# Feed-forward tiles moved to byte 288 of 512, and two weight halves exchanged between the ring of halves and the ends of the form tiles

## The chip, the cores and the metric

The kernel runs on one core of one Trainium2 chip. The metric is device time in microseconds; the kernel before takes 1804.18 us (median of 3 runs, 1803.63 to 1804.41).

## The reference

One encoder block over 256 tokens of width 2048. Two gated branches (a chunked linear attention and a Hyena convolution) are merged, projected and normalized; then comes the part that the change touches, a feed-forward layer with hidden width 8192:

```python
h  = _layernorm(ALPHA * h + mix, ln1_g, ln1_b)
ff = jnp.square(jax.nn.relu(h @ w_ff1)) @ w_ff2      # 2048 -> 8192 -> 2048
h  = _layernorm(ALPHA * h + ff, ln2_g, ln2_b)
```

All is float32 outside. Inside, each operand is split into a high part (rounded to the matmul format, made by ScalarE) and a low part (the rest, made by VectorE), and a product is taken as high x high + high x low + low x high.

## The kernel before

**Stages.** Input projections, the two branches, merging and output projection fill the first 1100 us. The feed-forward layer is cut into four quarters of 2048 hidden channels (16 blocks of 128 each).

- `ff1_first` makes the first quarter: 16 channel blocks `f0_*`. Each is one `[128 weights x 128]` load after the other, with the activations `hT` streamed past them (`channel_products`, lines 139 to 152): 8 products of 512 columns with the high half `h=0` (line 147), 16 of 256 columns with the low parts (line 151), and 8 of 512 with the high half `h=1`.
- `ff_pairs` is a loop of 48 iterations `s`. In each, TensorE forms the second layer's products of a finished pair of blocks (`form_products`, lines 1243 to 1245) and one channel block `f` of the next quarter. The second layer is taken by a seven-product scheme (quarters of the weight block are added up in pairs, and so are the activations). One iteration on TensorE, in order, is 9 products of the plain units (`w0` to `w2`), 6 of the pair (`w3`, `w4`), the channel block (8 + 16 + 8 products), then 6 of the last units (`w5`, `w6`) of the iteration before.
- Behind the loop, the last quarter's second layer is taken plainly (`token_products`, lines 199 to 201), with the activations as stationary operand, while `ff_close` finishes the seven-product sums.

**Operands of the products.** In a channel block the stationary operand is a weight half and the moving one is `hT`. In `form_products` the stationary operand is a slot of `fa[0]` or `fa[1]` (activation forms; four slots of 1792 floats each, slots 0 to 3 in `fa[0]`, 4 to 7 in `fa[1]`), and the moving one is a weight unit of 512 floats:

```python
for k, (wh, wl) in zip(ks, pieces_of.pop((p, which))):
    ps, f = pss[k], FORM[k]
    sh, sl = slot[:, 0, f], slot[:, 1, f]
    pin(MM(ps, sh, wh, start=(i == 0), stop=False))     # L1243
    MM(ps, sh, wl, start=False, stop=False)             # L1244
    pin(MM(ps, sl, wh, start=False, stop=(i == 7)))     # L1245
```

**Where the weights lie.** `weight_half(n, h)` takes a pair of tiles (`whi`, `wlo`, 1024 floats each) from a ring of three. In `ff_pairs` each iteration uses the ring three times: `half_split(s+1, 0)`, `pair_split(s+1)`, `half_split(s+1, 1)`. `plain_split` writes its units to `b_h` (tile `xh`) and `b_l` (tile `wx`). `last_split(s)` writes units 1 and 2, which POOL's accumulating DMAs have made into sums in the raw tile `ring`, to the ends `[:, 7168:8192]` of `fa[0]` (high) and `fa[1]` (low). VectorE's and ScalarE's order in the loop is written out by hand (`pin`). After the loop `fetch` puts blocks of the last quarter through the same ring; there the order is left to a planner.

The loop's body, in the order that is written out (lines 1286 to 1310):

```python
form_products(pss, s, 0, (0, 1, 2)); form_products(pss, s, 1, (3, 4))
ps = channel_psum(...)
for h in range(2): channel_products(ps, hT, half_parts.pop((s, h)), ...)
if s: form_products(pss, s - 1, 2, (5, 6))
if s + 2 < SLOTS: ring_load(s + 2)
if more: plain_split(s + 1); half_split(s + 1, 0); pair_split(s + 1)
...                                  # take_sums, squares, forms
quad_sum(n, c, ps, ...)              # low <- f on ScalarE, then fr <- f, f_l on VectorE
if more: half_split(s + 1, 1)
last_split(s)
```

**Addresses.** The pool `ep` lays its tiles one behind the other in the order in which their tags first appear: `bst` (384 bytes), `wx` (4096), `xh` and `xl` (8192 each), `f` (32768), `hT` (32768), then twelve buffers of 32 bytes for the norms' small columns (`mv`, `rs_y`, `rs_t`, `rs_v`, `lrs`, `lnb`, two each), then `fr3`, `fr4`, `ft`, `fraw`. The start of each large operand within a partition, modulo 512 bytes, follows:

| tile | start modulo 512 |
|---|---|
| `xT`, later `mT`, later `fa[0]`; `yT`, later `yg`, `yh` | 288 |
| `whi`, `wlo` (ring of halves), `raw`, `ring`, `dfth`, `eoh`, `Yh` | 32 |
| `hx` (Hyena filters) | 64 |
| `wx` (`b_l`), `xh` (`b_h`), `xl`, `f` (later `fa[1]`), `hT` | 416 |
| `fraw` | 288 |

All slots, units and weight columns used as operands lie at whole multiples of 512 bytes from these starts.

Of the kernel before, what the change touches and what calls it, by code (L numbers as in the profile page):

```python
# [9 lines left out]
F32 = mybir.dt.float32  # L10
# [6 lines left out]
P = 128  # L17
# [13 lines left out]
FF_PAIRS = W_OUT_END + 16  # L31
# [12 lines left out]
def block_kernel(  # L44
# [63 lines left out]
    def weight_half(n, h):  # L108
        return (wp.tile([P, D // 2], F32R, tag="whi", bufs=3, name=f"whi{n}_{h}"),
                wp.tile([P, D // 2], F32R, tag="wlo", bufs=3, name=f"wlo{n}_{h}"))  # L110
# [138 lines left out]
    with tc.tile_pool(name="xp", bufs=1) as xp, tc.tile_pool(name="xq", bufs=1) as xq:  # L249
# [25 lines left out]
        for i in range(3):  # L275
            t = weight_half(-1, i)
# [17 lines left out]
        for k0, n in PIECES:  # L294
# [13 lines left out]
            if k0 == 0:  # L308
                hi, lo = places[0]
# [165 lines left out]
    for i in range(2 * NCH):  # L475
        c, o = divmod(i, 2)
        n = 4 + (i * 21) // 15
# [421 lines left out]
    ep = ctx.enter_context(tc.tile_pool(name="ep", bufs=1))  # L899
# [4 lines left out]
    def load_rows(i0):  # L904
        rows = zr[:, 2:4]
        for i in range(2):
            nc.scalar.dma_start(rows[:, i, :], ln_rows[i0 + i:i0 + i + 1, :].broadcast_to([P, D]))
        return rows
# [54 lines left out]
                            MM(ps, sl, hi[:, cs], start=False, stop=(kt == KT - 1))  # L963

    st1 = ep.tile([P, NT, 8, 6], F32, tag="bst", name="bst1")
    rows1 = load_rows(0)
    turn_b, turn_i = dfth, dftl
    for i, t in ((0, turn_b), (1, turn_i)):
# [104 lines left out]
    fa = [base.tile([P, 8192], F32R, tag="xT", name="fa0"), None]  # L1073

    def fa_slot(i):
        if fa[1] is None:
            fa[1] = ep.tile([P, 8192], F32R, tag="f", name="fa1")
        t = fa[i // 4][:, i % 4 * 1792:(i % 4 + 1) * 1792]
        return t.rearrange("p (h k j) -> p h k j", h=2, j=P)
# [24 lines left out]
    def cast(hi, src):  # L1104
        return pin(nc.scalar.copy(hi, src))  # L1105

    def rest(lo, src, hi):
        return VT(lo, src, hi.bitcast(F32), ALU.subtract)
# [64 lines left out]
    def split_units(p, kind, hi, lo, raw):  # L1173
        by_unit = [t.rearrange("p (u c) -> p u c", c=512) for t in (hi, lo)]
        cast(by_unit[0], raw)
        rest(by_unit[1], raw, by_unit[0])
        pieces_of[p, kind] = list(zip(units(hi), units(lo)))

    def raw_units(p):
        return ring_tile(p).rearrange("p (u c) -> p u c", c=512)  # L1180
# [3 lines left out]
        split_units(p, 1, hi, lo, raw_units(p)[:, 0:4:3])  # L1184

    def last_split(p):
        fa_slot(4)
        hi, lo = (t[:, 7168:8192] for t in fa)
        split_units(p, 2, hi, lo, raw_units(p)[:, 1:3])

    block_raw = [None, None]
# [1 line left out]
    def block_load(p):  # L1193
        if block_raw[p % 2] is None:
            block_raw[p % 2] = ep.tile([P, D], F32, tag=("xl", "fraw")[p % 2], name=f"fraw{p}")
        nc.sync.dma_start(block_raw[p % 2], wblk[FF_PAIRS + 1 + 2 * p])
# [1 line left out]
    half_parts = {}  # L1198

    def half_split(p, h):  # L1200
        hi, lo = weight_half(FF_PAIRS + 1 + 2 * p, h)
        src = block_raw[p % 2][:, h * 1024:(h + 1) * 1024]
        cast(hi, src)
        rest(lo, src, hi)
        half_parts[p, h] = (hi, lo)
        if h and p + 2 < SLOTS:
            block_load(p + 2)
# [71 lines left out]
    def ff_pairs():  # L1279
        pss = [psum_side(f"w{j}") if j not in (2, 3, 4) else psum_main(f"w{j}") for j in range(7)]  # L1280
        joins = []
        for s in range(SLOTS):
# [12 lines left out]
            if more:  # L1295
                plain_split(s + 1)
                half_split(s + 1, 0)
# [9 lines left out]
            if more:  # L1307
                half_split(s + 1, 1)
            last_split(s)
            take_sums(pss, s - 1, (5, 6))  # L1310
            if s == SLOTS - 7:
# [32 lines left out]
    for h in range(2):  # L1344
        half_split(0, h)
# [58 lines left out]
    with tc.high_priority(), tc.issue_after(done.ins):  # L1404
        add_ff(pss[1][:, 0:256], 1, 1792, 256, last=True)
        mv = ep.tile([P, 2], F32, tag="mv", bufs=2, name="mvl")
        nc.vector.bn_aggr(mv, st2[:, 1])
        y, t, v, rs = (ep.tile([P, 1], F32, tag=f"fin{i}", name=f"fin{i}") for i in range(4))
# [158 lines left out]
```

## Time and profile before

| | |
|---|---|
| median of 3 runs | 1804.18 us |
| the profiled execution | 1803.89 us |
| its span | 1802.1 us |
| granted TensorE clock | 0.999 |
| busy: TensorE / VectorE / ScalarE / POOL | 1793.6 / 1455.6 / 1039.2 / 164.6 us |

Times in the profile count from the start of the span. In the profile PE is the stream of matmuls and PEld that of weight loads; DVE is VectorE and ACT ScalarE. The mean of one matmul in a group counts from its start to its modelled end, and neighbours overlap in it. The chain of waits counts from one start to the next. A name like `w<-b_h,fa` is output, moving operand, stationary operand.

### The profile page before, as it was taken

What the parts mean: (1) busy time and instruction counts of PE and PEld (TensorE: products, weight loads), DVE (VectorE), ACT (ScalarE), POOL (GpSimd) and SP (SyncE); (2) the same over time, 40 slices, a digit from 0 to 9 for tenths busy, and PEclk for the clock granted to TensorE, in tenths of its full rate; (3) what the DMA queues carried; (4) which work ended last, traced back from release to release, by engine and by line L of the source; (5) the groups of instructions that cost most, each with busy time, mean ns of one, the idle gap of its engine ahead of it and who ended that gap; (6) DMA issues with size and microseconds to landing.
All of it is one profiled execution on the core that took longest, in us unless ns stands there. A gap on an engine that the chain in (4) does not pass through costs nothing.

```text
span 1802.1 us, 23458 instructions
## 1 busy us (share of the span) xinstructions
PE 1793.6 (100%) x8787; PEld 1506.8 (84%) x8787; DVE 1455.6 (81%) x1869; ACT 1039.2 (58%) x1399; POOL 164.6 (9%) x217
## 2 busy tenths in 40 slices
PE   9999999999999999999999999999999999999998
PEld 7888888888888888888888889888888888888887
DVE  6789887875679989998845568687899889999867
ACT  6678768875344444445544445666667666665632
POOL 1011110000111101010000000001111111111100
PEclk9999999999999999999999999999999999999999
DMA  8668775455797979798555764568888888888663
GB/s 325 231 248 293 253 234 196 149 179 197 224 311 247 276 261 285 232 309 257 202 187 187 283 236 155 203 192 258 243 252 255 249 243 261 247 240 276 212 222 119
DMA packets 79281, 424.76 MB, mean 236 GB/s; under 512 B 9816, under 2 KB 12392, under 8 KB 38464
## 3 DMA queue, kind: packets, MB, share of 16 engines
q1 hardware_dynamic: 47808, 336.61, 50.5%
q0 software_dynamic: 24304, 66.99, 18.1%
q10 hardware_dynamic: 7056, 19.67, 3.0%
q8 instruction: 69, 1.13, 0.3%
q14 instruction: 44, 0.36, 0.1%
HBM read 381.86 MB, written 16.25 MB: 221 GB/s over the span
## 4 chain that ended last, share of the span: by engine, by line
PE 97%; DVE 2%; issue 0%; ACT 0%; DVEq 0%; ACTq 0%
PE f L147 12%; PE f L151 6%; PE w L1244 4%; PE w L1243 4%; PE w L1245 4%; PE g L200 3%; PE g L199 3%; PE g L201 3%; PE ux L200 3%; PE ux L199 3%; PE ux L201 3%; PE r L199 2%; PE r L200 2%; PE r L201 2%; PE k L147 2%; PE v L200 2%
## 5 line engine op out<-in xcount | busy, mean ns | idle before, releaser
L86 ACT CAST whi<-raw 128x1024 fp32r<-128x1024 f32 x392 | 412.5, 1053 | 412.9 <-PE ux L201 85.1
L87 DVE TENSOR_TENSOR wlo<-raw,whi 128x1024 fp32r<-128x1024 f32 x392 | 478.4, 1223 | 206.9 <-ACT whi L86 204.6
L147 PE MATMUL f<-hT,whi 128*128 128x512 f32 x984 | 246.9, 395 | 0.4 <-DVE fr L1102 0.4
L147 PEld LDWEIGHTS f<-hT,whi 128*128 128x128 f32 x984 | 180.7, 188 | 38.8 <-DVE fr L1102 0.8
L151 PEld LDWEIGHTS f<-hT,wlo 128*128 128x128 f32 x984 | 125.4, 188 | 5.6
L1102 DVE TENSOR_TENSOR wlo<-fraw,whi 128x1024 fp32r<-128x1024 f32 x96 | 117.3, 1222 | 13.5 <-ACT whi L1105 11.2
L151 PE MATMUL f<-hT,wlo 128*128 128x256 f32 x984 | 127.0, 282 | 0.0
L1105 ACT CAST whi<-ring 128x1024 fp32r<-128x1024 f32 x48 | 50.6, 1054 | 101.0 <-DVE ring L1102 97.6
L1168 POOL DMA_DIRECT2D ring<-wblk x48 | 41.7, 868 | 706.9 <-DVE ring L1102 706.9
L1105 ACT CAST whi<-fraw 128x1024 fp32r<-128x1024 f32 x96 | 100.7, 1049 | 0.1
L200 PE MATMUL g<-wlo,xT 128*128 128x512 f32 x256 | 100.2, 391 | 0.0
L201 PE MATMUL ux<-whi,xT 128*128 128x512 f32 x256 | 99.9, 390 | 0.0
L201 PE MATMUL g<-whi,xT 128*128 128x512 f32 x256 | 99.9, 390 | 0.0
L200 PE MATMUL ux<-wlo,xT 128*128 128x512 f32 x256 | 99.7, 389 | 0.0
L199 PE MATMUL g<-whi,xT 128*128 128x512 f32 x256 | 93.8, 392 | 0.0
L1105 ACT CAST b_h<-ring 128x1024 fp32r<-128x1024 f32 x96 | 75.2, 832 | 25.9 <-PE w L1245 21.5
L199 PE MATMUL ux<-whi,xT 128*128 128x512 f32 x256 | 89.7, 389 | 0.0
L1102 DVE TENSOR_TENSOR b_l<-ring,b_h 128x1024 fp32r<-128x1024 f32 x48 | 58.7, 1223 | 16.0 <-ACT b_h L1105 15.9
L1102 DVE TENSOR_TENSOR ring<-ring 128x512 f32<-128x512 f32 x96 | 66.2, 689 | 1.5
L1102 DVE TENSOR_TENSOR wlo<-ring,whi 128x1024 fp32r<-128x1024 f32 x48 | 58.8, 1225 | 1.9 <-ACT whi L1105 0.3
L1102 DVE TENSOR_TENSOR fa<-ring,fa 128x1024 fp32r<-128x1024 f32 x48 | 58.5, 1220 | 0.0
L1169 POOL DMA_DIRECT2D ring<-ring x48 | 58.1, 1210 | 0.0
(537 smaller groups left out, 4305.9 us busy)
## 6 DMA issues: line engine op xcount, KB each, us to landing
raw<-wblk SPq DMA_DIRECT2D x204, 1024.0 KB, 5.0
fraw<-wblk SPq DMA_DIRECT2D x48, 1024.0 KB, 4.8
ring<-wblk SPq DMA_DIRECT2D x48, 1024.0 KB, 7.1
Td<-T POOLq DMA_DIRECT2D x32, 384.0 KB, 5.4
conv_sb<-conv_rows SPq DMA_DIRECT2D x12, 1024.0 KB, 11.5
Tl<-Td POOLq DMA_DIRECT2D x16, 768.0 KB, 9.5
ring<-wblk POOLq DMA_DIRECT2D x48, 256.0 KB, 4.4
ring<-ring POOLq DMA_DIRECT2D x48, 256.0 KB, 5.1
```

Source lines behind the costliest of these rows:

```text
L86: return (nc.scalar.copy(hi, src), nc.vector.tensor_tensor(lo, src, hi.bitcast(F32), op=ALU.subtract))
L87: nc.vector.tensor_tensor(lo, src, hi.bitcast(F32), op=ALU.subtract))
L147: MM(ps[:, :, ts], hi[:, js], act[:, kt, :, ts], start=(kt == 0 and opens), stop=(kt == KT - 1))
L151: MM(ps[:, 0, ts], lo[:, js], act[:, kt, 0, ts], start=False, stop=False)
L199: MM(pss[tb], sh, wh, start=(kt == 0), stop=False)
L200: MM(pss[tb], sh, wl, start=False, stop=False)
L201: MM(pss[tb], sl, wh, start=False, stop=(kt == KT - 1))
L1102: return pin(nc.vector.tensor_tensor(dst, a, b, op=op))
L1105: return pin(nc.scalar.copy(hi, src))
L1243: pin(MM(ps, sh, wh, start=(i == 0), stop=False))
L1244: MM(ps, sh, wl, start=False, stop=False)
L1245: pin(MM(ps, sl, wh, start=False, stop=(i == 7)))
```

## The change

Two edits. The first creates the twelve small buffers of the norms ahead of the large tiles of `ep` (behind `bst`), without any instruction: they take 12 x 32 = 384 bytes there, and everything from `wx` to `hT` starts 384 bytes later, at 288 modulo 512. The tiles behind them stay where they were. The second exchanges two places: `half_split(p, 1)`, the second half of a channel block's weights, goes to the ends of `fa[0]` and `fa[1]`, and `last_split(p)`, the DMA-made sums, goes to the ring of halves.

```diff
     st1 = ep.tile([P, NT, 8, 6], F32, tag="bst", name="bst1")
+    for tag, n in (("mv", 2), ("rs_y", 1), ("rs_t", 1), ("rs_v", 1), ("lrs", 1), ("lnb", 1)):
+        ep.tile([P, n], F32, tag=tag, bufs=2, name=f"first_{tag}")
     rows1 = load_rows(0)
...
     def last_split(p):
-        fa_slot(4)
-        hi, lo = (t[:, 7168:8192] for t in fa)
+        hi, lo = weight_half(FF_PAIRS + 2 * p, 1)
         split_units(p, 2, hi, lo, raw_units(p)[:, 1:3])
...
     def half_split(p, h):
-        hi, lo = weight_half(FF_PAIRS + 1 + 2 * p, h)
+        fa_slot(4)
+        hi, lo = (t[:, 7168:8192] for t in fa) if h else weight_half(FF_PAIRS + 1 + 2 * p, h)
         src = block_raw[p % 2][:, h * 1024:(h + 1) * 1024]
         cast(hi, src)
         rest(lo, src, hi)
```

No instruction is added or removed, and the order of the calls stays.

## The prediction, made before the changed kernel was built

> **What bounds the kernel now.** I read the page first: busy times, clock, chain of waits.
>
> ```profile
> span 1802.1 us, 23458 instructions
> PE 1793.6 (100%) x8787; PEld 1506.8 (84%) x8787; DVE 1455.6 (81%) x1869; ACT 1039.2 (58%) x1399; POOL 164.6 (9%) x217
> PE 97%; DVE 2%; issue 0%; ACT 0%; DVEq 0%; ACTq 0%
> ```
>
> TensorE is the bound: it is busy for 1793.6 of 1802.1 us at a clock of 0.999, and 97% of the chain is PE. There is next to no idle time to win, so a gain must come from matmuls that follow each other more closely. Whether they can is asked of the groups of instructions with shapes kept apart (x count, busy, mean ns of one), for one and the same form, 128x128 weights and 512 columns:
>
> ```profile
> L199 PE MATMUL go<-whi,yg 128*128 128x512 f32 x128 | 46.6, 389 | 0.0
> L333 PE MATMUL yp<-Yh,dfth 128*128 128x512 f32 x32 | 12.5, 389 | 0.0
> L330 PE MATMUL X<-hx,eoh 128*128 128x512 f32 x32 | 12.7, 397 | 0.0
> L147 PE MATMUL f<-hT,whi 128*128 128x512 f32 x984 | 246.9, 395 | 0.4 <-DVE fr L1102 0.4
> L1243 PE MATMUL w<-b_h,fa 128*128 128x512 f32 x144 | 56.7, 394 | 0.0
> L1245 PE MATMUL w<-b_h,fa 128*128 128x512 f32 x144 | 56.4, 391 | 0.0
> L1244 PE MATMUL w<-b_l,fa 128*128 128x512 f32 x96 | 37.8, 394 | 0.0
> L1243 PE MATMUL w<-whi,fa 128*128 128x512 f32 x96 | 37.7, 393 | 0.0
> L1244 PE MATMUL w<-wlo,fa 128*128 128x512 f32 x96 | 37.9, 395 | 0.0
> L1245 PE MATMUL w<-whi,fa 128*128 128x512 f32 x96 | 37.6, 392 | 0.0
> L1243 PE MATMUL w<-fa 128*128 128x512 f32 x48 | 19.1, 398 | 0.0
> L1243 PE MATMUL w<-fa,fa 128*128 128x512 f32 x48 | 18.6, 392 | 0.0
> L1244 PE MATMUL w<-fa,fa 128*128 128x512 f32 x48 | 19.0, 395 | 0.0
> L1244 PE MATMUL w<-fa 128*128 128x512 f32 x48 | 18.7, 390 | 0.0
> L1245 PE MATMUL w<-fa 128*128 128x512 f32 x48 | 18.9, 394 | 0.0
> L1245 PE MATMUL w<-fa,fa 128*128 128x512 f32 x48 | 18.8, 392 | 0.0
> L199 PE MATMUL w<-whi,fa 128*128 128x512 f32 x96 | 34.3, 393 | 0.0
> L201 PE MATMUL w<-whi,fa 128*128 128x512 f32 x96 | 37.6, 392 | 0.0
> ```
>
> Set the table of addresses beside these rows. In `go`, moving (`whi`, 32) and stationary operand (`yg`, 288) start 256 bytes apart modulo 512: 389 ns. In `yp` both start at 32: 389 again. In `X` they differ by 32 bytes (64 and 32): 397. The feed-forward groups mix 416 with 32, 288 and 416, so most pairs differ by 128 modulo 256, and their means lie between 390 and 398. Equal modulo 256 reads as fast, anything else as slow, and the slow `X` stands in an early stage, far from the feed-forward loop. The mean contains a tail that overlaps the next matmul. The chain of waits has starts alone; here is a channel block of `f` against one of `q`, the same instructions with `xT` (288) in place of `hT` (416):
>
> ```profile
> 1162.19 1.90 PE f L151 x16
> 1164.10 3.72 PE f L147 x16
> ...
> 48.91 2.73 PE q L147 x12
> 51.64 1.91 PE q L151 x16
> 53.55 1.84 PE q L147 x8
> ```
>
> A block of `f` is 3.72/2 + 1.90 + 3.72/2 = 5.62 us. For `q`, eight products before the low parts are 2.73 x 8/12 = 1.82, then 1.91 and 1.84: 5.57 us. The low parts gain nothing (1.91 against 1.90), and behind them the high products take a while to close up (1.84 against 1.82).
>
> **The change part by part.** *The shift by 384 bytes.* It brings `wx`, `xh`, `f` (with it `fa[1]`) and `hT` from 416 to 288. Afterwards every moving and stationary operand of the feed-forward part starts at 32 or 288, so every pair is 0 or 256 bytes apart. No instruction comes or goes, nothing is queued differently, and the small tiles are off the path. Terms, as an excess over 389 ns:
>
> - Plain units (`b_h`, `b_l`): 144 x 5 + 144 x 2 + 96 x 5 = 1488 ns, and for the last 48 of the 432 (L1244, not shown) the same mean of 3.9: 1674 ns.
> - Pair units (`whi`, `wlo` at L1243 to L1245): 96 x (4 + 6 + 3) = 1248 ns.
> - Last units (`w<-fa`, six rows): 48 x (9 + 3 + 6 + 1 + 5 + 3) = 1296 ns. These need both edits: today their high part is at 288 and their low part at 416; in the ring both would be at 32.
> - Channel blocks: 48 in the loop and 13 whole ones before it, 61 x (5.62 - 5.57) = 3.05 us.
> - Last quarter: 96 x (4 + 3) for L199 and L201, half as much again for L200 between them: 1008 ns. The mean there mixes `fa[0]`, at 288 already, with `fa[1]`.
>
> The sum is 1.67 + 1.25 + 1.30 + 3.05 + 1.01 = 8.3 us.
>
> By the Trainium skill (TensorE: Matmul & The Clock Gate, Part 2, step by step) loading the next weights does not steal read bandwidth from the running matmul, as the two come through separate ports; by it the sum would be zero. The rows 389 and 397 of one form at one clock speak against that here.
>
> *The exchange.* `half_split(s+1, 1)` and `last_split(s)` keep their places in the orders of ScalarE, VectorE and SP. The ends of `fa` and one buffer of the ring swap roles: the half is freed by the block's last products, the last units by the six products behind it, as before, each having one buffer. So in the loop no wait is added, and POOL's sums and the load that SP issues behind `half_split(s+1, 1)` go out as they did. The weights of `h=1` now lie at 288 against `hT` at 288, the case of `yp` (389), not of `go`. Between 0 and the worst row of the stage, 398, I take 389; equal starts are what `yp` shows.
>
> *What the loop gives back.* VectorE has little room in the loop, so I looked for where it already holds TensorE up. The chain of waits leaves PE once for long, and the windows of single iterations show two long ones:
>
> ```profile
> 1513.89 0.06 DVE wlo L1102
> ...
> 1558.37 2.12 PE f L147 x8
> ```
>
> ```profile
> 1554.32:1565.50 11.18, 10.76 (x55) 8.78 (x54) 10.55 (x15) 7.15 (x10) 2.26 (x4) 1.00 0.72 218
> 1638.80:1649.61 10.81, 10.77 (x54) 8.78 (x53) 10.73 (x13) 7.26 (x10) 3.32 (x4) 1.00 0.83 254
> 1208.62:1691.51 482.89, 482.43 (x2439) 407.19 (x2438) 433.45 (x536) 317.20 (x415) 82.11 (x94) 1.00 0.83 251
> ```
>
> The columns of a window are its length, then the busy time (and count) of PE, PEld, DVE, ACT and POOL, the clock, the DMA share and GB/s. The third window holds 46 iterations of 10.50 us. From 1513.89 to 1558.37 the chain runs over VectorE and what feeds it: 44.5 us, 4.2 iterations, at whose end TensorE waited (11.18 - 10.50 = 0.68; the row of `f` above names `fr`). That stretch is VectorE's to set, so what TensorE wins in it is waited away. The loop's share of the gain is 1.67 + 1.25 + 1.30 + 48 x 0.05 = 6.6 us, 0.138 an iteration: 4.2 x 0.138 = 0.6 us lost. The other long one, 0.31 over 10.50, has VectorE busy for 10.73; if the two iterations ahead of it are as tight, it grows alike: 3 x 0.138 = 0.4. On the mean VectorE is busy for 433.45/46 = 9.42 against a new iteration of 10.36, so elsewhere it keeps up. Loss 1.0 us; its bounds are 0 (slack that I don't see) and 3.0 (the waits of VectorE on ScalarE add up and twice as many iterations as today are VectorE's).
>
> *Behind the loop.* There the ring matters: the last units of iteration 47 sit in it, so the block after the next is one buffer short.
>
> ```profile
> 1701.06 1.05 ACT L86 CAST whi<-raw 128x1024 fp32r<-128x1024 f32 x1
> ...
> 1706.26 1.06 ACT L86 CAST whi<-raw 128x1024 fp32r<-128x1024 f32 x1 [0.93 <-PE w L201]
> ```
>
> ```profile
> 1707.35 1.22 DVE L87 TENSOR_TENSOR wlo<-raw,whi 128x1024 fp32r<-128x1024 f32 x1
> ...
> 1717.80 0.69 DVE L1276 SCALAR_TENSOR_TENSOR zr<-zr 128x512 f32<-128x512 f32 x1
> ```
>
> ```profile
> 1707.42 0.62 PE L199 MATMUL w<-whi,fa 128*128 128x512 f32 x2
> ```
>
> The half that is split at 1701.06 today, in the buffer of `h=1`, moves to the slot at 1706.26, where it waits for the first half of the running block; its low part would be there at 1708.57, and TensorE asks for it from about 1707.42. Queued behind that cast on ScalarE are the following casts, on VectorE the closing sums and forms. With the six closing products put first (each 1.86/8 = 0.23, together 1.4 us) nothing is lost, without them about 1.15 us. I take 0.3.
>
> **Sum.** 8.3 - 1.0 - 0.3 = 7.0 us. Against the profiled execution, 1803.89 us, that is 1796.9; the median of the runs is 0.29 higher, 1804.18, which gives 1797.2 us. About 0.2% (3.6 us) is what a measurement of this kernel can tell from no change.
>
> **The rivals.**
>
> *A. Addresses do nothing.* The excess comes from the loop's own traffic on SBUF (two splitting engines, DMA at 0.83), not from the operands' starts. For it: the slow groups are nearly all in this stage. Against it: `X` with 397 outside it, and the last quarter's `fa` rows, 392 to 393, behind the loop. Time: 1804.2 plus up to 1.15 behind the loop, about 1804.5. The Trainium skill (SBUF — State Buffer, Who interferes with whom) has TensorE wait for no one, which would rule out this traffic as well as the gain. Chance 0.05.
>
> *B. Equal starts collide.* Pairs 256 bytes apart run at 389, pairs 0 apart at the 398 of `w<-fa`, whose high unit is at 288 against `fa[0]` at 288. For it: that row. Against it: `yp`. Price: plain units (432 products, mean 392.9) lose 5.1 each, 2.2 us; the half `h=1` of 48 blocks loses 384 x 3 = 1.2 us; `h=0` gains 6 x 488 = 2.9; pairs 1.25, last units 1.30 and the last quarter 1.01 stay. That leaves 3.1 us, less 0.4 in the loop and 0.3 behind it: about 1801.8. Chance 0.07.
>
> *C. A half stuck behind the closing sums.* VectorE works in order, and its last closing sum ends at 1718.49. If the planner puts the low part of the displaced half behind it, TensorE stands until about 1719.7 instead of 1707.4: 12 us against 7.3 won (8.3 - 1.0), so 1804.18 + 4.8 = 1809.0, slower. It decides from a stall of 7.3 us on. Against it: today's order alternates splits with single sums. Chance 0.03.
>
> **How the numbers follow.** Forecast 0.85; A 0.05; B 0.07; C 0.03. The forecast's own range: best 8.3 with nothing lost and half a nanosecond of rounding on 2,300 products (1.1 us), 1794.8; worst 8.3 - 1.1 - 3.0 - 1.15 = 3.05, about 1801.1. That range also comes within 0.7 us of B, and leaves out A, B and C, 0.15. Faster by over 0.2% (under 1800.6): 0.84, nearly all of the forecast. Within 0.2%: 0.12 (A, B and the rest). Slower: 0.04.
>
> **What would show it.** Right: `f<-hT,whi` falls from 395 to 391 (as in a block of 5.57 us), and `w` rows to 389 or 390; an ordinary iteration lasts 10.36 us, and all seven sums' products look alike. The long iterations stay long: 11.2 and 10.8 become about 11.7 and 11.1. VectorE's share of the chain of waits rises above 2%, and behind the loop TensorE idles less than 1.2 us. Wrong: `f` at 395 or above in the half whose weights are in `fa` (B), both halves unchanged (A), one gap of several microseconds near 1705 (C), or a chain that runs over VectorE through most of the loop, so that the iterations stay at 10.45 although the matmuls' means have fallen.

## The result and the profile after

The changed kernel takes 1796.46 us in the median of five runs (1795.53 to 1797.93), against 1804.17 for the kernel before beside it (1803.63 to 1804.41): the ratio is 0.9957, with a 95% interval of 0.9944 to 0.9971. The forecast was 1797.2. The kernel is faster by 7.7 us, and the interval of the ratio excludes 1.

The profiled execution is the slowest of the five, 1797.93 us. First its page: span, busy times, and the shares of the chain of waits.

```profile
span 1796.2 us, 23460 instructions
PE 1785.1 (99%) x8787; PEld 1507.0 (84%) x8787; DVE 1453.7 (81%) x1869; ACT 1038.0 (58%) x1399; POOL 164.7 (9%) x217
PE 93%; DVE 3%; DMA 1%; ACT 1%; issue 1%; SPq 0%; ACTq 0%; DVEq 0%
```

TensorE runs the same 8787 matmuls in 8.5 us less of busy time. The counts of all five engines in this line are as before (the two instructions more in the span are semaphore instructions); the matmuls follow each other more closely. The groups with shapes kept apart say which (the lines of the loop are two higher than before, 1245 to 1247 in place of 1243 to 1245):

```profile
L199 PE MATMUL go<-whi,yg 128*128 128x512 f32 x128 | 46.6, 389 | 0.0
L330 PE MATMUL X<-hx,eoh 128*128 128x512 f32 x32 | 12.7, 397 | 0.0
L147 PE MATMUL f<-hT,whi 128*128 128x512 f32 x600 | 146.6, 390 | 1.1 <-DVE fr L1104 1.1
L147 PE MATMUL f<-hT,fa 128*128 128x512 f32 x384 | 96.2, 392 | 0.0
L1246 PE MATMUL w<-wlo,fa 128*128 128x512 f32 x192 | 74.8, 390 | 0.5 <-DVE wlo L1104 0.5
L199 PE MATMUL w<-whi,fa 128*128 128x512 f32 x96 | 33.9, 389 | 0.0
```

`go` and `X`, whose tiles didn't move, read 389 and 397 as before. Every `w` row of the loop, spread over 390 to 398 before, is now at 389 or 390. The 1.1 us in the row of `f` and the 0.5 in that of `w` are TensorE's waits on VectorE, of which before's page had 0.4. Stretches of the trace show where the time came from. The rows are windows of before (the channel blocks ahead of the loop, 47 iterations, and from the last iteration's start to the last matmul), then of after, where a window of 46 iterations and the two long ones stand between:

```profile
1124.56:1199.53 74.97, 74.97 (x427) 65.34 (x425) 53.77 (x78) 45.89 (x69) 1.80 (x2) 1.00 0.60 206
1199.53:1691.51 491.98, 491.52 (x2486) 414.93 (x2485) 441.31 (x548) 324.07 (x425) 82.58 (x94) 1.00 0.82 249
1691.51:1796.78 105.27, 104.43 (x503) 86.63 (x502) 79.75 (x111) 41.45 (x49) 0.00 (x0) 1.00 0.49 173
```

```profile
1126.38:1200.59 74.21, 74.21 (x427) 65.50 (x425) 54.85 (x79) 46.74 (x69) 1.80 (x2) 1.00 0.61 209
1200.59:1686.81 486.22, 484.61 (x2487) 415.26 (x2485) 439.59 (x547) 322.34 (x424) 82.61 (x94) 1.00 0.83 251
1209.56:1686.81 477.25, 475.64 (x2440) 407.52 (x2438) 432.69 (x536) 316.31 (x415) 81.89 (x94) 1.00 0.84 254
1550.36:1562.10 11.74, 10.62 (x55) 8.78 (x54) 11.06 (x16) 7.62 (x11) 2.79 (x4) 1.00 0.71 211
1634.38:1645.50 11.12, 10.63 (x54) 8.79 (x53) 11.05 (x13) 7.50 (x10) 3.23 (x4) 1.00 0.79 234
1686.81:1790.83 104.02, 103.17 (x503) 86.60 (x502) 79.72 (x112) 41.64 (x49) 0.00 (x0) 1.00 0.49 175
```

The blocks ahead of the loop give 74.97 - 74.21 = 0.76 us, the loop 491.98 - 486.22 = 5.76, the end 105.27 - 104.02 = 1.25: 7.77 together. The spans of the two profiles differ by less, 5.9, because this execution came to the channel blocks 1.82 us later (1126.38 against 1124.56). Most of that is one wait in the opening, the first row here of TensorE's waits (us in total, times, longest):

```profile
PE open L289 <- ACT whi-1_2_133 L301: 1.2, 1, 1.2
PE f L147 <- DVE fr L1104: 1.1, 1, 1.1
```

A second profile of the changed kernel, from an experiment below, doesn't have that wait, and has the loop at 486.21 us. For differences of about 1 us the windows are therefore the better measure.

### The profile page after: what moved, and what is told of

The parts are those of the page before. It is cut to its first block, busy times and chain, and to the rows that moved or that the text cites. A ratio compares the mean times of both kernels' runs of the same rounds, so it can differ in the third digit from the quotient of the medians.

```text
span 1796.2 us, 23460 instructions
## 1 busy us (share of the span) xinstructions
PE 1785.1 (99%) x8787; PEld 1507.0 (84%) x8787; DVE 1453.7 (81%) x1869; ACT 1038.0 (58%) x1399; POOL 164.7 (9%) x217
## 4 chain that ended last, share of the span: by engine, by line
PE 93%; DVE 3%; DMA 1%; ACT 1%; issue 1%; SPq 0%; ACTq 0%; DVEq 0%
PE f L147 11%; PE f L151 6%; PE w L1246 4%; PE w L1247 4%; PE w L1245 4%; PE g L200 3%; PE g L199 3%; PE g L201 3%; PE ux L199 3%; PE ux L201 3%; PE ux L200 3%; PE r L199 2%; PE r L201 2%; PE r L200 2%; PE k L147 2%; PE v L200 2%
## 5 line engine op out<-in xcount | busy, mean ns | idle before, releaser
L1107 ACT CAST whi<-ring 128x1024 fp32r<-128x1024 f32 x96 | 101.1, 1053 | 103.1 <-DVE ring L1104 102.6
L147 PE MATMUL f<-hT,whi 128*128 128x512 f32 x600 | 146.6, 390 | 1.1 <-DVE fr L1104 1.1
L147 PEld LDWEIGHTS f<-hT,whi 128*128 128x128 f32 x600 | 111.7, 188 | 24.1 <-DVE fr L1104 1.5
L1104 DVE TENSOR_TENSOR wlo<-ring,whi 128x1024 fp32r<-128x1024 f32 x96 | 117.2, 1221 | 1.9 <-ACT whi L1107 0.3
L147 PE MATMUL f<-hT,fa 128*128 128x512 f32 x384 | 96.2, 392 | 0.0
L151 PE MATMUL f<-hT,wlo 128*128 128x256 f32 x600 | 81.6, 282 | 0.0
L147 PEld LDWEIGHTS f<-hT,fa 128*128 128x128 f32 x384 | 69.1, 189 | 12.3
L1246 PE MATMUL w<-wlo,fa 128*128 128x512 f32 x192 | 74.8, 390 | 0.5 <-DVE wlo L1104 0.5
L1247 PE MATMUL w<-whi,fa 128*128 128x512 f32 x192 | 74.7, 389 | 0.0
L1245 PE MATMUL w<-whi,fa 128*128 128x512 f32 x192 | 74.6, 389 | 0.0
L1104 DVE TENSOR_TENSOR fa<-fraw,fa 128x1024 fp32r<-128x1024 f32 x48 | 58.7, 1224 | 13.1 <-ACT fa L1107 10.7
```

The costliest lines, as they stand in the source:

```text
L147: MM(ps[:, :, ts], hi[:, js], act[:, kt, :, ts], start=(kt == 0 and opens), stop=(kt == KT - 1))
L151: MM(ps[:, 0, ts], lo[:, js], act[:, kt, 0, ts], start=False, stop=False)
L1104: return pin(nc.vector.tensor_tensor(dst, a, b, op=op))
```

## The experiments

Each was run five times, beside the kernel before, unless it says otherwise. Two theories were at issue first: that the gain is the starting addresses (T), and that it is something that came along with them, in the order, in the buffers or in the other engines' traffic.

**The shift alone.** `half_split` and `last_split` stay as before.

```diff
     st1 = ep.tile([P, NT, 8, 6], F32, tag="bst", name="bst1")
+    for tag, n in (("mv", 2), ("rs_y", 1), ("rs_t", 1), ("rs_v", 1), ("lrs", 1), ("lnb", 1)):
+        ep.tile([P, n], F32, tag=tag, bufs=2, name=f"first_{tag}")
```

> The first edit alone: the large tiles start 384 bytes later, the two places stay as before the change. Theory T (the gain is the starting addresses, pairs that start equal modulo 256 bytes follow each other faster): every pair of the feed-forward part is 0 or 256 bytes apart here too, because fa[1]'s end moves to 288 with it. So f<-hT,whi and f<-hT,fa read 390 to 392, every w row 389 or 390, and the time is the changed kernel's, 1796.5 us within 0.7. Rival (the prediction's own claim that the last units need both edits): their term of 1.3 us is missing, six rows of w of the last units stay at 390 to 398, about 1797.8 us.

Measured: 1796.27 us (1796.10 to 1797.56), ratio 0.9957 (0.9944 to 0.9969). Its groups:

```profile
L147 PE MATMUL f<-hT,whi 128*128 128x512 f32 x984 | 242.7, 391 | 1.1 <-DVE fr L1104 1.1
L1245 PE MATMUL w<-fa 128*128 128x512 f32 x48 | 18.7, 389 | 0.0
L1246 PE MATMUL w<-fa,fa 128*128 128x512 f32 x48 | 18.7, 389 | 0.0
```

All of the gain is here, and all six rows of the last units read 389, these two among them. The prediction's "these need both edits" is refuted: the shift takes `fa[1]`'s end from 416 to 288 by itself. The first row also answers case B. Here both halves' weights are at 32 against `hT` at 288; in the changed kernel the second half is at 288 against 288, and its two rows, 600 at 390 and 384 at 392, have a mean of 390.8, against 391 here. So 0 apart is as good as 256 apart, and the 392 is not a collision.

The exchange isn't quite without effect. The 47 iterations and one of them, in the shift alone:

```profile
1199.55:1686.39 486.84, 484.85 (x2486) 415.15 (x2485) 440.93 (x548) 323.57 (x425) 82.58 (x94) 1.00 0.83 251
1528.65:1539.59 10.94, 10.58 (x54) 8.78 (x53) 10.87 (x14) 6.03 (x8) 1.76 (x3) 1.00 0.77 232
```

The loop is 0.62 us longer than the changed kernel's, all of it in an iteration in which VectorE is busy for 10.87 us. The planner orders VectorE's free work anew for each kernel; whether that or the exchange itself makes the difference was not tried, and the total, 0.2 us lower, doesn't show it.

**The exchange alone.**

```diff
     def last_split(p):
-        fa_slot(4)
-        hi, lo = (t[:, 7168:8192] for t in fa)
+        hi, lo = weight_half(FF_PAIRS + 2 * p, 1)
...
     def half_split(p, h):
-        hi, lo = weight_half(FF_PAIRS + 1 + 2 * p, h)
+        fa_slot(4)
+        hi, lo = (t[:, 7168:8192] for t in fa) if h else weight_half(FF_PAIRS + 1 + 2 * p, h)
```

> The second edit alone: the two places are exchanged, the large tiles stay at 416 modulo 512. Theory T: hT at 416 against whi at 32 and against fa[0]'s end at 288 and fa[1]'s at 416, so f<-hT,whi stays near 395 and f<-hT,fa reads 395 for its high parts; the last units now pair 32 with 288 or 416, and gain at most half of their excess, 0.6 us. Time 1803.5 to 1804.2 us. Rival (the exchange itself carries a part of the gain, by order or by freeing buffers earlier): 1802 us or less. Rival (the exchange costs behind the loop, as the prediction had it, up to 1.15 us): up to 1805.3 us.

Measured: 1804.25 us in eleven runs (1803.25 to 1805.73), ratio 1.0000 (0.9991 to 1.0009). One of its groups, and its 47 iterations:

```profile
L147 PE MATMUL f<-hT,fa 128*128 128x512 f32 x384 | 97.0, 395 | 0.0
```

```profile
1198.63:1690.90 492.27, 492.04 (x2486) 415.47 (x2485) 439.95 (x547) 323.61 (x424) 82.75 (x94) 1.00 0.82 248
```

The exchange gains nothing: 492.27 in the loop against 491.98 before, and `f`, whose `hT` stays 128 bytes from the weights in `fa[0]`, stays at 395.

**Another shift, by 128 bytes.** The large tiles land at 32 in place of 288.

```diff
-    for tag, n in (("mv", 2), ("rs_y", 1), ("rs_t", 1), ("rs_v", 1), ("lrs", 1), ("lnb", 1)):
+    for tag, n in (("mv", 2), ("rs_y", 1)):
```

> The change, with the large tiles at 32 modulo 512 in place of 288 (a shift by 128 bytes in place of 384). Theory T: every pair is again 0 or 256 bytes apart, only with the two swapped: f<-hT,whi pairs 32 with 32. Rows of f at 390 to 392 and w at 389 or 390, time 1796.5 us within 0.7. Rival 1 (equal starts collide, the prediction's case B): the pairs with whi and the ring go to 396 to 398, 1801 us or more. Rival 2 (288 itself is what is good): no gain at all, about 1804 us.

Measured: 1796.70 us (1796.09 to 1796.97), ratio 0.9957 (0.9944 to 0.9969).

Its two rows of `f` equal the changed kernel's above digit for digit (390 and 392), although the two halves have changed roles: here `hT` and `whi` are 0 apart, `hT` and `fa[0]`'s end 256. So what counts is neither the address 288 nor whether the distance is 0 or 256. The second half has one thing in common in both kernels, its place behind the 256-column low parts. The starts of the single matmuls in the traces show what that does: in both kernels its eight products follow each other in 233, 236, 228, 232 or 233, 231 and then 227 ns (medians over the iterations), so after five of them they are as close as the rest.

**A shift by 160 bytes.** The two tiles of the last experiment and one more of 32 bytes:

```diff
-    for tag, n in (("mv", 2), ("rs_y", 1), ("rs_t", 1), ("rs_v", 1), ("lrs", 1), ("lnb", 1)):
+    for tag, n in (("mv", 2), ("rs_y", 1)):
...
+    ep.tile([P, 8], F32, tag="gap2", name="gap2")
```

> The change, with the large tiles at 64 modulo 512, so 32 bytes off the weights' buffers modulo 256. Theory T in its strict form (only a difference of 0 modulo 256 is fast): f and w rows at 394 to 398 like X<-hx,eoh, whose operands are 32 bytes apart (397), in every pair, also in those that were 0 or 256 apart before the change; time 1804 to 1809 us. Rival (only a difference of 128 modulo 256 hurts, and X is slow for a reason of its own): as the changed kernel, 1796.5 us within 0.7.

Measured: 1803.66 us in eleven runs (1802.48 to 1804.92), ratio 0.9996 (0.9987 to 1.0004).

```profile
L147 PE MATMUL f<-hT,whi 128*128 128x512 f32 x600 | 150.1, 395 | 0.3 <-DVE fr L1105 0.3
L147 PE MATMUL f<-hT,fa 128*128 128x512 f32 x384 | 97.3, 395 | 0.0
L1246 PE MATMUL w<-whi,fa 128*128 128x512 f32 x192 | 75.9, 396 | 0.0
```

With the operands 32 bytes apart the gain is gone, all of it, as it was with 128 before. The expected 1804 to 1809 was missed by 0.3 us on the near side: 32 apart is no worse than 128. The expectation also had every pair apart, which isn't so: the plain units (64) start equal to the slots in `fa[1]` (64), and the ring's units (32) 256 away from the slots in `fa[0]` (288). In the kernel before these two groups start equal modulo 256 as well (416 and 416, 32 and 288). That the whole gain is gone all the same has a reason in the starts of single matmuls, here the medians over the iterations. The nine plain units on `fa[1]` come 231 ns apart and then 227 or 226, but the six pair units on `fa[0]`, at equal starts too, come 234, 229, 231, 231, 236 and 228 apart behind products that don't start equal. So a run of products at equal starts takes a few of them to reach 227 ns, and a short run between unequal ones doesn't get there. One and the same pair reads 398 in the kernel before (`w<-fa`, L1243 in the prediction's rows, 288 against 288 with the slots in `fa[0]`) and 389 in the shift alone, where its neighbours start equal too.

**The cost by itself.** This one ran once.

```diff
+    def run(name, n, w0, off):
+        ps = mmp.tile([P, 512], F32, tag="mm", name=name)
+        for k in range(64):
+            a = w0 + 128 * (k % 8)
+            m = 2048 + w0 + off
+            tc.keep_in_program_order(
+                MM(ps[:, 0:n], big[:, a:a + 128], big[:, m:m + n], start=(k == 0), stop=(k == 63)))
```

> The disputed cost by itself: this kernel leaves the whole computation out, and only runs groups of 64 matmuls, 128x128 weights and 512 columns, all with the same data, where the moving operand's start differs from the weights' start by 0, 8, 16, 32, 64, 96, 128, 192, 256, 384 or 512 bytes modulo 512 (a group's name says which: by_half is 128, by_full 256), then two groups with both starts moved together, three of 256 columns, and the first once more. No other engine works beside them, and no DMA. Theory T (the difference of the starts modulo 256 bytes sets how closely matmuls follow): 0, 256 and 512 apart read 389 and the group lasts 64 x 0.227 = 14.5 us; every other difference reads 394 to 398 and lasts 14.8 to 15.2; moving both together changes nothing. Rival A (traffic of other engines and DMAs on the same memory, not the starts): all groups alike, 14.5 us, as nothing else runs. Rival B (only with other traffic do the starts matter): likewise all alike.

In the chain of waits (start, length, what) each group is one piece. The distances are, from the top, 0, 8, 16, 32, 64, 96, 128, 192, 256, 384 and 512 bytes, then 0 with both starts moved by 64 and by 128, then 256 columns at distances of 0 and 64, and 512 columns at 0 once more:

```profile
41.21 14.51 PE by_zero L90 x64
55.72 14.95 PE by_eight L90 x64
70.66 14.82 PE by_sixteen L90 x64
85.49 14.93 PE by_thirtytwo L90 x64
100.42 14.65 PE by_sixtyfour L90 x64
115.07 14.93 PE by_ninetysix L90 x64
130.00 14.93 PE by_half L90 x64
144.93 14.92 PE by_halfandmore L90 x64
159.85 14.55 PE by_full L90 x64
174.40 14.93 PE by_fullandhalf L90 x64
189.32 14.52 PE by_twofull L90 x64
203.84 14.55 PE both_sixtyfour L90 x64
218.39 14.56 PE both_half L90 x64
232.95 7.68 PE narrow_zero L90 x64
240.63 7.54 PE narrow_sixtyfour L90 x64
...
255.76 14.54 PE again_zero L90 x64
```

But for one ScalarE copy of 0.59 us behind each group, nothing runs beside these matmuls, and all groups take the same data at a granted clock of 1.00. Starts that are equal modulo 256 give 14.51 to 14.56 us, 227 ns a matmul, also when both are moved together; 8, 32, 96, 128, 192 and 384 apart give 14.92 to 14.95, 233 ns; 16 apart, 14.82, is a little better. Rivals A and B fall: the other engines' traffic isn't needed. The strict form of T is nearly right; 64 apart, at 14.65, keeps two thirds of the gain, which T didn't have, and 192, which is 64 the other way round, keeps none. The few hundredths between the groups at equal starts go by what ran ahead: `by_zero`, behind another equal group, comes at 227 ns from its first matmul, `again_zero` (behind 256 columns at 128) after three and `by_full` (behind 192) after ten. With 256 columns there is nothing to gain; equal starts are the slowest of the three distances tried (128 apart gives 7.59).

**Where the loop gives some of it back.** The two long iterations were 11.18 and 10.81 before and are 11.74 and 11.12 now. Theory V: VectorE is behind in both, at the first by the forms of two iterations in a row beside a group's closing sums, at the second by joins that the planner gathers. One experiment for each.

```diff
-                joins.pop(0)()
+                pin(joins.pop(0)())
```

> The changed kernel, but the joining of the parts of a sum, one piece per iteration, is held at its place in VectorE's order, where the planner otherwise gathers several of them ahead of the iteration that starts at 1634.4 us. Theory V (the two long iterations are waits on VectorE, made by what is gathered there): the iteration of 11.12 us falls to about 10.33, the one of 11.74 stays, the time is 0.8 us less than the changed kernel's, 1795.7 us. Rival (TensorE waits there for the loads or for ScalarE): both long iterations stay, 1796.5 us.

Measured: 1795.52 us (1794.89 to 1797.18), ratio 0.9954 (0.9942 to 0.9967).

```profile
1548.10:1559.85 11.75, 10.62 (x54) 8.79 (x53) 11.08 (x16) 7.62 (x11) 2.77 (x4) 1.00 0.71 217
1632.14:1642.46 10.32, 10.32 (x54) 8.86 (x53) 9.26 (x11) 7.48 (x11) 1.76 (x2) 1.00 0.88 264
```

The second is gone: VectorE is busy for 9.26 us in it, in place of 11.05. The first stays. The 46 iterations last 476.46 us, 0.79 less than the changed kernel's 477.25, as expected. In the other experiment four forms of each eight go one iteration later:

```diff
-    FORMED = {16 * (q - 1) + s: 8 * q + i for q in range(1, 4) for i, s in enumerate((10, 11, 13, 14, 16, 17, 19, 20))}
+    FORMED = {16 * (q - 1) + s: 8 * q + i for q in range(1, 4) for i, s in enumerate((10, 11, 13, 14, 17, 18, 20, 21))}
```

> The changed kernel, but the four later ones of each group of eight forms are made one iteration later, so that in the iteration that starts at 1550.4 us VectorE has not the forms of two iterations and the closing sums of a group behind one another. Theory V: the iteration of 11.74 us falls to about 10.33 to 10.6, the one of 11.12 stays; time 1.1 to 1.4 us less than the changed kernel's, 1795.1 to 1795.4 us. Rival (the wait is for the loads or for ScalarE): 11.74 stays, 1796.5 us. Rival (the forms only wait one iteration more and stall TensorE there): another iteration becomes as long, 1796.5 us.

Measured: 1794.99 us (1794.34 to 1795.87), ratio 0.9951 (0.9938 to 0.9963).

```profile
1528.86:1539.80 10.94, 10.57 (x54) 8.79 (x53) 10.87 (x14) 6.03 (x9) 1.76 (x3) 1.00 0.74 234
1550.13:1560.46 10.33, 10.33 (x55) 8.86 (x53) 9.69 (x15) 7.40 (x11) 1.42 (x3) 1.00 0.78 229
1632.88:1643.43 10.55, 10.55 (x54) 8.79 (x53) 10.48 (x13) 7.01 (x10) 3.22 (x4) 1.00 0.85 248
```

The first long iteration is gone, and the second nearly (10.55). In exchange the one at 1528.86, two ahead of the first, lasts 10.94, with VectorE busy for 10.87, the third case of such an iteration; so the rival of another long iteration came true in part. With the joins held as well it is gone (below). The 46 iterations last 476.01 us, 1.24 less. The other rivals (loads, ScalarE) fall in both cases: the loads and the casts are the same, and the waits are gone. The totals of these two runs lie within each other's intervals and the changed kernel's; it is the windows that decide.

**The filters' operands.** `X` is the early group at 397, its operands 32 apart.

```diff
-        mc = fp.tile([P, 4], F32, tag="mlpc", name="mlpc")
+        mc = fp.tile([P, 64], F32, tag="mlpc", name="mlpc")[:, 0:4]
```

> The changed kernel, with one small tile ahead of the position filters' operands made wider, so that X's moving operand hx moves from 64 to 288 modulo 512 against its weights at 32, 256 apart in place of 32. Theory T: X<-hx,eoh falls from 397 to 389 or 390, as the only early stage where a 128x512 row is slow; 96 products of X by 5 to 7 ns and the filters' 128x256 ones by up to 4 ns: 0.5 to 0.9 us less than the changed kernel's, 1795.6 to 1796.0 us. Rival (X is slow for its place in the program, not for its addresses): 397 stays, 1796.5 us.

Measured: 1796.96 us (1794.74 to 1797.90), ratio 0.9961 (0.9948 to 0.9975). By the time nothing can be said. By the rows, one of 512 columns and one of 256:

```profile
L330 PE MATMUL X<-hx,eoh 128*128 128x512 f32 x32 | 12.5, 390 | 0.0
...
L333 PE MATMUL X<-h,eoh 128*128 128x256 f32 x32 | 9.0, 283 | 0.0
```

`X` falls from 397 to 390, at its old place in the program; the place isn't what made it slow. The 256-column rows don't fall as expected, this one rises from 279 to 283. The window of this stage, from the first product of `X` to the last, is 172.17 us, against 173.63 in the kernel with the later forms, where TensorE doesn't wait in it either: the wider tile gives 1.46 us there.

**All three together.**

> The changed kernel with all three: joins held at their places, four forms one iteration later, filters' operands at 288. If the terms add: 0.8 + 1.2 + 0.7 = 2.7 us less than the changed kernel's, 1793.8 us (1793 to 1794.5); no iteration of the loop over 10.6 us, X at 389 or 390. Rival (the stalls are not VectorE's and X is not the addresses'): 1796.5 us.

Measured: 1793.09 us (1792.79 to 1794.32), ratio 0.9941 (0.9929 to 0.9954). The terms add. To tell the parts apart, three kernels were run on one chip: the changed one, the one with both edits to VectorE's order, and this one.

> The changed kernel itself once more, beside the next two on one chip: 1796.5 us within 0.7, whatever the theory.

> The changed kernel with the joins held at their places and four forms an iteration later, without the wider tile ahead of the filters. If the two terms measured singly add, 2.2 us less than the changed kernel's on the same chip (1.4 for the forms, 0.8 for the joins), 1794.3 us. Rival (they stand in each other's way in VectorE's order): no better than the forms alone, 1795.0 us.

> The same with the wider tile too, so that X and the filters' products have both operands' starts equal modulo 256. Theory T: 0.5 to 0.9 us less than without it, 1793.1 to 1793.8 us; singly the term was lost in the scatter of the runs. Rival (its gain in X is waited away in the early stage): no less than without it.

Measured: 1796.39 (1795.99 to 1797.69), 1794.69 (1793.69 to 1795.65) and 1793.20 us (1792.23 to 1793.54), with ratios of 0.9959 (0.9946 to 0.9973), 0.9949 (0.9937 to 0.9961) and 0.9939 (0.9927 to 0.9952). The runs of the first and the last don't overlap: this version beats the changed kernel by 3.2 us and the kernel before by 10.7. In windows, 46 iterations and the stretch from the first product of `X` to the last, first without the wider tile, then the stretch with it (the 46 iterations last 475.13 there):

```profile
1208.32:1683.46 475.14, 475.14 (x2440) 407.49 (x2438) 431.27 (x532) 316.81 (x415) 81.89 (x94) 1.00 0.83 253
89.06:263.73 174.67, 174.02 (x821) 144.63 (x820) 154.74 (x209) 130.03 (x166) 18.05 (x30) 1.00 0.75 256
```

```profile
89.04:261.33 172.29, 172.29 (x821) 144.87 (x820) 154.52 (x209) 130.66 (x166) 18.03 (x30) 1.00 0.76 260
```

The loop falls from 477.25 to 475.14: 2.1 of the 2.2 us expected, and TensorE is busy for all of it, an ordinary 10.33 on the mean. The early stretch loses 1.7 us of busy time here, and 1.5 between the two kernels compared for the filters' operands above; 0.5 to 0.9 was expected. `X` itself accounts for 0.6 (three rows of 32, lower by 7, 4 and 7 ns). Most of the rest is in products whose own addresses didn't change, those that run between the ones of `X`; first without and then with the wider tile:

```profile
L201 PE MATMUL r<-whi,xT 128*128 128x512 f32 x128 | 50.1, 391 | 0.0
```

```profile
L201 PE MATMUL r<-whi,xT 128*128 128x512 f32 x128 | 49.8, 389 | 0.0
```

Between the two kernels compared above, the three rows of `r` give 0.75 us from start to start and those of `v` 0.18, and the 256-column ones of `X` cost 0.15. The operands of `r` started equal modulo 256 all along (32 and 288); it is their neighbours that do so now.

## Why the prediction was right, point by point

**The terms.** The mechanism is shown: the shift alone brings the gain, two shifts that make the starts equal modulo 256 bring the same, one that doesn't brings none, and the matmuls alone show it with nothing beside them. The rule of the Trainium skill (TensorE: Matmul & The Clock Gate, Part 2), that loading the next weights takes no read bandwidth from the running matmul, gave a sum of zero. The measurement decides: 14.51 against 14.93 us for 64 matmuls, by the operands' starts alone. The prediction's reading that equal modulo 256 is fast and anything else slow needs an addition: the row of a pair depends on its neighbours too, as the shift by 160 bytes shows. Its terms came out all the same, because they were taken as the excess of the measured rows, of equal and unequal pairs together. What exactly meets what inside, no run here shows.

**The sizes.** The blocks ahead of the loop gave 0.76 us, where 13 x 0.05 = 0.65 was counted. A block in the chain is now 3.65/2 + 1.91 + 3.65/2 = 5.56 us:

```profile
1163.60 1.91 PE f L151 x16
1165.51 3.65 PE f L147 x16
```

An ordinary iteration was forecast at 10.36 and lasts 10.33. Most of that is the 10.50 from which 0.138 was taken: that mean contained the two long iterations. Without them it is (482.89 - 11.18 - 10.81)/44 = 10.475, and after it is (477.25 - 11.74 - 11.12)/44 = 10.327, so the gain is 0.148 an iteration, 7% above the forecast. From start to start in the traces, the plain units give 0.035 of it and the pair units 0.026, both as forecast; the last units give 0.031 (forecast 0.027) and the channel block 0.056 (0.05).

**The claim on the last units** failed, as told: one edit does it. Its 1.30 us was in the sum and came, so the time didn't suffer; but the exchange, to which it was put down in part, is worth nothing that the time can tell.

**The loss in the loop.** Forecast: iterations of about 11.7 and 11.1, 1.0 us lost. Measured: 11.74 and 11.12, that is 1.41 + 0.79 over 10.33, where it was 0.70 + 0.34 over 10.475: 1.16 us lost. That VectorE makes both is shown by the two experiments that take its work elsewhere. Its share of the chain rose from 2% to 3%, as said.

**Behind the loop** 0.3 us was set aside for a half that might wait for its slot. There was none: the list of TensorE's waits behind the last iteration's start has one entry, 0.8 us in the last closing step, which the kernel before has as well. The end gave 1.25 us, the last quarter's 1.01 and what an iteration gains, with nothing taken off. Case C didn't happen.

**The sum.** 7.77 us in the windows against 7.0: 0.1 more ahead of the loop, 0.2 more inside it net, 0.5 more behind it (0.3 that wasn't lost, the rest the last iteration, counted in the loop's term). Case A is refuted by the shifts, B by the shift by 128 bytes.

## What to carry to other kernels

Where TensorE is busy throughout and rows of one matmul form differ by a few nanoseconds, set the operands' starting addresses beside the rows, and make moving and stationary starts equal modulo 256 bytes by the order in which tiles are created; here up to 2.6% in start-to-start time (233 against 227 ns in the matmuls alone) and 0.4% of the whole, for no instruction. Do it for all products that follow one another: an equal pair between unequal ones stays partly slow, and setting one group right speeds up its neighbours. Then look in windows of single iterations for the engine that the faster loop now waits for: the gain is lost where that engine's work piles up, and spreading it is the next gain. For differences under 1 us read the stage's window, as the total scatters by more.

## What the runs showed of the hardware that was not expected

With nothing else running, 512-column matmuls follow each other in 227 ns when the operands start equal modulo 256 bytes and in 233 when they are 8, 32, 96, 128 or 192 bytes apart; 16 apart (232) and 64 apart (229) lie between, and 64 apart the other way round (192) does not. 256-column ones don't gain: 7.68 us for 64 at a distance of 0, 7.54 at 64. And a matmul's spacing depends on what ran ahead of it too: behind products of unequal starts or of 256 columns, a run at equal starts took between one and ten matmuls to come down to 227 ns. So the second half of a channel block reads 392 behind the narrow products, 0 apart in one kernel and 256 apart in the other, where the rest of the block reads 390, and `r` fell from 391 to 389 when its neighbours `X` were put right.
